# Moving the x chain's weight pool from the left side of SBUF to the right end

## The chip, the core and the metric

The kernel runs on one core of one Trainium2 chip. The metric is the device time of one execution in microseconds; less is better. Before the change the median of three executions is 1627.95 us (1626.01 to 1629.65). The profile was taken of one further execution.

## The reference

A block of two layers (a mixer of windowed attention and a state space model, then sparse attention) on x, 256 tokens of width 1024, is followed by a block of two layers in which x attends to a context `ctx` of 256 tokens. In the second block both streams are normalised and modulated by a conditioning vector, and each layer ends in a gated feed-forward of width 2816; the second layer's mixer is a bidirectional SSM. All is float32. Cut to what matters here:

```
h = x
for layer in range(2):                       # first block, x alone
    hn = rms_norm(h, norm_g[layer])
    h = h + (even_layer if layer == 0 else odd_layer)(hn, ...)   # hn @ w_in ... @ w_out
x = h
for i in range(2):                           # second block, x and ctx
    h, hc = modulate(x, ...), modulate(ctx, ...)
    y, yc = attention_mixer(h, hc, ...) if i == 0 else ssm_mixer(h, hc, ...)
    x = x + g1 * y
    x = x + g2 * swiglu(modulate(x, ...), w_gate, w_up, w_down)
    if i == 0:
        ctx = ctx + cg1 * yc
        ctx = ctx + cg2 * swiglu(modulate(ctx, ...), w_gate, w_up, w_down)
return rmsnorm(x, final_norm_g)
```

Nearly all of the arithmetic is in products of a 256 x 1024 (or 2816, or 2048) activation with a weight matrix that is read once from DRAM.

## The kernel before

**Two chains.** The x chain (both blocks) and the ctx chain (its attention, its feed-forward, and its part of the SSM layer) are written as one program, and a scheduler interleaves them by priority. Each chain has its own weight pool, its own activation pools and its own PSUM tiles: `psx` for x (PSUM banks 0 to 3), `psc` for ctx (banks 4 to 7).

**Weights.** A `Weights` object (L156) is a pool with three kinds of buffer, each 128 partitions x 1024 float32, so 4096 bytes in each partition: `raw` for what a DMA of the SP queue brings (`fetch`, L167), and `h` and `l`, the two halves of the number in the rounded format of TensorE. `load` (L175) makes `h` on ScalarE (L181) and `l = raw - h` on VectorE (L182), now and then on GpSimd. `wx`, the x chain's pool, has 3 raw, 2 h and 2 l buffers: 7 x 4096 = 28672 bytes in a partition. `wc`, the ctx chain's, has 2 of each: 24576 bytes. Activations are split the same way into a pair of tiles (`nhx`/`nlx` the normalised x, `nhc`/`nlc` the normalised ctx, `fh`/`fl` the inner activations of a feed-forward, `yH`/`yL`, `oHx`/`oLx`, `ysH`/`ysL` the outputs of the mixers), and a product is the sum of three matmuls: high x high, low x high, high x low.

**Which operand is loaded.** TensorE holds one operand (128 columns, loaded by LDWEIGHTS) and streams the other past it. In the profile `out<-a,b` is a matmul that streams `a` past the loaded `b`. There are two forms:
- `feat_tiles` (L273) loads a 128 x 128 slice of the weights and streams 256 tokens of activation: `pffnx<-nhx,h` (gate and up products of the x feed-forwards, 24 matmuls for each tile of weights), `pcvx` (SSM input products; for three of four channel tiles also with `nhc`/`nlc` streamed past the same x weights), `pg` (gates of the first block, 16 tiles), and a few more (`pu`, `pqi`, `pki`, `pglu`, 14 tiles together). `pffnc<-nhc,h` is the same of the ctx feed-forward, with weights of `wc`.
- `tok_step` (L232) loads a slice of activation and streams 512 or 256 columns of weights: `pdx<-h,nhx`, `pdx<-h,fh`, `pdx<-h,ysH` and so on for x, `pdc<-h,nhc`, `pdc<-h,oHc`, `pdc<-h,fh` for ctx. The outputs `pdx` lie in `psx`, apart from half of the product with `ysH`/`ysL`, which lies in `psc`.

`step_sizes` (L1216) is a small case of the first form, with 64 weight columns in place of 128 (`pdt`, in `psx` for x).

**Order of the program around the change.** The scheduler's order is fixed when the program is built. The pools are stacks: left pools grow from byte 0 of each partition, right pools from the end. On the left stand `con`, `res`, `act`, `wk`, then `wx`, `xw` and one pool for each stage of the x chain (`ev`, `od`, `l0`, `ff0`, `l1`, `ff1`); on the right `wc`, then `cx`, which are closed by `cst.close()` (L1479) ahead of the x chain's SSM stage, whose pool `l1` then grows over their place. Start bytes in each partition, of the built program before:

| tile | pool | start byte |
|---|---|---|
| `nhx`, `yH`, `oHx` | act | 36512 |
| `nlx`, `yL`, `oLx` | act | 44704 |
| `nhc`, `oHc` | act | 52896 |
| `nlc`, `oLc` | act | 61088 |
| first buffer of `wx` | wx | 70048 |
| `fh`, `fl` of x | ff0, ff1 | 115104, 126368 |
| `ysH`, `ysL` | l1 | 115232, 131616 |
| `fh`, `fl` of ctx | cx | 165664, 191264 |
| first buffer of `wc` | wc | 204768 |

The other buffers of `wx` and `wc`, and the slices of 128 or 256 columns of any of these tiles, follow at multiples of 512 bytes from these starts.

Of the kernel before, what the change touches and what calls it, by code (L numbers as in the profile page):

```python
# [47 lines left out]
WX = (3, 2)  # L48
WC = (2, 2)
# [42 lines left out]
def build(tc, A):  # L92
    nc = tc.nc
    T, V, S, G, SY = nc.tensor, nc.vector, nc.scalar, nc.gpsimd, nc.sync
    es = ExitStack()
# [8 lines left out]
    def pool(name, bufs=1, space=None, right=False):  # L104
        kw = {"side": "right"} if right else {}
        if space is not None:
            kw["space"] = space
        else:
            kw["reuse_waits"] = "tile"
        return tc.tile_pool(name=name, bufs=bufs, **kw)  # L110
# [5 lines left out]
    class Banks:  # L116
        def __init__(self, name, bufs):
            self.p = es.enter_context(pool(name, 1, PS))
            self.bufs = bufs
            self.k = name[2]  # L120
# [33 lines left out]
    flip = misc[:, 420:548]  # L154

    class Weights:  # L156
        def __init__(self, name, raw, hl, eng, right=False):
            self.p = (cst if right else es).enter_context(pool("w" + name, raw, right=right))
            self.hl = hl
            self.eng = eng  # L160

            self.ahead = []
            self.n = 0
            self.name = name
            self.on_pool = 0
# [21 lines left out]
    def cols(a, ncols, n0, k0=0, kt=8):  # L187
        return [(lambda t: t, dram(a, k0 * 128 * ncols + n0, [[ncols, 128], [128 * ncols, kt], [1, 128]]))]

    wx = Weights("x", *WX, SY)  # L190
    cst = ExitStack()
    wc = Weights("c", *WC, SY, right=True)
    cx = cst.enter_context(pool("cx", right=True))
    xw = es.enter_context(pool("xw"))
    xpool = {"x": (xw, "xn"), "c": (cx, "cfl")}
# [1312 lines left out]
```

## Time and profile before

| | |
|---|---|
| median of three executions | 1627.95 us (1626.01 to 1629.65) |
| profiled execution | 1627.45 us |
| its span, first to last instruction | 1625.4 us |
| mean granted TensorE clock | 0.973 of full |
| PE busy | 94% of the span |
| VectorE, ScalarE, GpSimd busy | 68%, 46%, 19% |
| DMA | 264.58 MB, mean 163 GB/s |

The span lies 2.05 us under the execution's own time, and that under the median by 0.50 us. PE is TensorE's matmuls, PEld its weight loads, which overlap them; DVE is VectorE, ACT ScalarE, POOL GpSimd, SP the queue that issues the DMAs. Matmuls are pipelined: the length that the profile gives to one is longer than the distance from one start to the next, and it is the distance that adds up to time.

### The profile page before, as it was taken

To read this page: it belongs to the slowest core of one execution; us is meant where nothing else is said; L and a number is where in the kernel's file an instruction comes from. 1 tells how busy PE (TensorE), PEld (TensorE's weight loads), DVE (VectorE), ACT (ScalarE), POOL (GpSimd) and SP (SyncE) were. 2 spreads that over 40 slices of the span, in tenths; PEclk is the share of its full clock that TensorE was granted. 3 is DMA by queue.
4 is the path that set the end of the run, shared out by engine and by line. 5 is a ranking of instruction groups with operands and counts; after the bars stand their busy time and mean duration, and the time that the engine had idled before them with its cause. 6 is when DMAs were issued, how large, how long until landed. Compare 5 with 4: busy or idle time off the path is not lost.

```text
span 1625.4 us, 27122 instructions
## 1 busy us (share of the span) xinstructions
PE 1524.9 (94%) x10660; PEld 1307.0 (80%) x10660; DVE 1104.7 (68%) x1823; ACT 745.3 (46%) x1336; POOL 301.8 (19%) x260
## 2 busy tenths in 40 slices
PE   6989987999999999999999999887999999899998
PEld 5655664786998988888889897787899889699997
DVE  6789776567766676655666565569888787655666
ACT  3412256545544544666444343433454444444443
POOL 4476420000100100000000000129454430100000
PEclk9989998999999999999999999889999999999999
DMA  8755574466656656423665766334444433555664
GB/s 264 216 183 170 167 202 138 124 179 209 185 178 205 197 175 194 138 79 95 200 206 183 235 185 204 99 90 131 106 119 117 113 97 114 162 162 176 192 185 136
DMA packets 302735, 264.58 MB, mean 163 GB/s; under 512 B 27329, under 2 KB 256495, under 8 KB 302608
## 3 DMA queue, kind: packets, MB, share of 16 engines
q1 hardware_dynamic: 301680, 259.70, 53.5%
q0 software_dynamic: 928, 3.15, 0.7%
q8 instruction: 84, 1.38, 0.3%
q14 instruction: 43, 0.35, 0.1%
HBM read 261.47 MB, written 1.34 MB: 162 GB/s over the span
## 4 chain that ended last, share of the span: by engine, by line
PE 77%; DVE 7%; DMA 7%; POOL 5%; issue 2%; ACT 1%; SPq 1%; POOLq 0%; DVEq 0%; ACTq 0%
PE pdx L132 21%; PE pffnx L132 16%; PE pffnc L132 8%; PE pdc L132 7%; PE pcvx L132 6%; PE pada L905 3%; DMA araw<-ada_w 2%; PE pg L132 2%; PE py L132 2%; PE pl0x L132 1%; POOL EW L1372 1%; PE pl1x L132 1%; PE pocx L132 1%; PE ptcx L1086 1%; DVE l L182 1%
## 5 line engine op out<-in xcount | busy, mean ns | idle before, releaser
L182 DVE TENSOR_TENSOR l<-raw,h 128x1024 fp32r<-128x1024 f32 (+2 forms) x362 | 452.9, 1254 | 284.8 <-ACT h L181 231.1
L181 ACT ACTIVATE h<-raw 128x1024 fp32r<-128x1024 f32 (+2 forms) x374 | 389.2, 1042 | 487.3 <-PE pdx L132 147.5
L132 PE MATMUL pffnx<-nhx,h 128*128 128x256 f32 x704 | 174.9, 286 | 0.0
L132 PE MATMUL pffnx<-nlx,h 128*128 128x256 f32 x704 | 174.7, 285 | 0.2 <-DVE nlx L352 0.2
L132 PEld LDWEIGHTS pffnx<-nhx,h 128*128 128x128 f32 x704 | 136.5, 194 | 1.2 <-issue 1.2
L132 PEld LDWEIGHTS pffnx<-nlx,h 128*128 128x128 f32 x704 | 136.3, 194 | 1.0 <-DVE nlx L352 0.9
L310 POOL TENSOR_TENSOR sums<-sums,nhalf 128x1 f32<-128x1 f32 x20 | 14.6, 730 | 559.0 <-DVE sums L306 542.0
L132 PE MATMUL pffnx<-nhx,l 128*128 128x256 f32 x704 | 99.0, 283 | 0.0
L905 PE MATMUL pada<-araw,cT 128*32 128x256 f32 x704 | 76.3, 403 | 18.5 <-DMA araw<-ada_w 18.5
L132 PEld LDWEIGHTS pffnx<-nhx,l 128*128 128x128 f32 x704 | 91.1, 193 | 0.0
L132 PE MATMUL pffnc<-nhc,h 128*128 128x256 f32 x352 | 87.1, 285 | 0.0
L132 PE MATMUL pcvx<-nhx,h 128*128 128x256 f32 x256 | 77.3, 309 | 9.3 <-DVE cv L1257 9.3
L182 POOL TENSOR_TENSOR l<-raw,h 128x1024 fp32r<-128x1024 f32 (+1 forms) x12 | 27.3, 2277 | 315.7 <-PE pdx L132 202.2
L132 PE MATMUL pffnc<-nlc,h 128*128 128x256 f32 x352 | 85.5, 281 | 0.0
L132 PE MATMUL pdx<-h,nhx 128*128 128x256 f32 (+1 forms) x256 | 83.6, 345 | 0.4 <-DVE cv L1257 0.4
L132 PE MATMUL pdx<-h,nlx 128*128 128x256 f32 (+1 forms) x256 | 80.7, 334 | 0.0
L132 PE MATMUL pdx<-h,fh 128*128 128x256 f32 (+1 forms) x264 | 78.8, 323 | 0.0
L132 PE MATMUL pdx<-h,fl 128*128 128x256 f32 (+1 forms) x264 | 77.8, 319 | 0.0
L132 PE MATMUL pcvx<-nlx,h 128*128 128x256 f32 x256 | 75.3, 302 | 0.0
L132 PEld LDWEIGHTS pffnc<-nhc,h 128*128 128x128 f32 x352 | 66.4, 189 | 2.8 <-issue 1.2
L132 PEld LDWEIGHTS pffnc<-nlc,h 128*128 128x128 f32 x352 | 66.4, 189 | 0.8 <-DVE ss L408 0.4
L132 PEld LDWEIGHTS pcvx<-nhx,h 128*128 128x128 f32 x256 | 51.8, 203 | 13.3 <-issue 13.1
(600 smaller groups left out, 3892.4 us busy)
## 6 DMA issues: line engine op xcount, KB each, us to landing
araw<-ada_w SPq DMA_DIRECT2D x88, 512.0 KB
raw<-ffn_w_gate SPq DMA_DIRECT2D x66, 512.0 KB
raw<-ffn_w_up SPq DMA_DIRECT2D x66, 512.0 KB
raw<-ffn_w_down SPq DMA_DIRECT2D x54, 512.0 KB
raw<-ssm_w_in SPq DMA_DIRECT2D x48, 512.0 KB
raw<-od_w_in SPq DMA_DIRECT2D x25, 512.0 KB
raw<-attn_w_qkv SPq DMA_DIRECT2D x24, 512.0 KB
raw<-attn_w_o SPq DMA_DIRECT2D x32, 256.0 KB
```

Source lines behind the costliest of these rows:

```text
L132: i = T.matmul(out, l, r, start=start, stop=stop)
L181: S.activation(h[:, :n], raw[:, :n], AF.Copy)
L182: (G if self.on_pool > 0 else V).tensor_tensor(l[:, :n], raw[:, :n], h[:, :n].bitcast(F32), op=ALU.subtract)
L310: G.tensor_tensor(s[:, 3:4], s[:, j - 1:j], nhalf[:, 0:1], op=ALU.pow)
L905: T.matmul(pt[32 * q:32 * q + 32, 0:256], cT[:, k, :], raw[:, q * 256:(q + 1) * 256], start=k == 0, stop=k == 7, tile_position=(0, 32 * q))
L1086: T.transpose(pt[:, e, r], P[:, e, r, ki * 128:(ki + 1) * 128], ident)
L1372: (G if CWP else V).tensor_tensor(EW, E, W, op=ALU.mult)
```

## The change

`wx` becomes a right pool, opened before `wc`, so that it takes the last 28672 bytes of the partition; `wc` and `cx` stand left of it. `wx` stays open to the end of the kernel, on the stack `es`; `wc` is closed with `cst` as before.

```diff
@@ -154,8 +154,8 @@
     class Weights:
-        def __init__(self, name, raw, hl, eng, right=False):
-            self.p = (cst if right else es).enter_context(pool("w" + name, raw, right=right))
+        def __init__(self, name, raw, hl, eng, stack):
+            self.p = stack.enter_context(pool("w" + name, raw, right=True))
             self.hl = hl
             self.eng = eng
@@ -187,9 +187,9 @@
-    wx = Weights("x", *WX, SY)
     cst = ExitStack()
-    wc = Weights("c", *WC, SY, right=True)
+    wx = Weights("x", *WX, SY, es)
+    wc = Weights("c", *WC, SY, cst)
     cx = cst.enter_context(pool("cx", right=True))
```

In the built program no instruction, no place in any engine's order and no wait differs: only the start bytes of SBUF tiles do. `con`, `res`, `act` and `wk` stay. The first buffer of `wx` goes from byte 70048 to byte 200672. Every other tile (the x chain's `xw` and stage pools, `wc` and `cx`) moves down by 28672 bytes, so that what overlapped of `l1` and the closed ctx pools overlaps as before.

## Rows read from the trace of the kernel before

**Rows 1.** The page, busy time by engine: us, share of the span, instructions.

```profile
PE 1524.9 (94%) x10660; PEld 1307.0 (80%) x10660; DVE 1104.7 (68%) x1823; ACT 745.3 (46%) x1336; POOL 301.8 (19%) x260
```

**Rows 2.** The page, the chain that ended last: shares of the span by engine and line.

```profile
PE 77%; DVE 7%; DMA 7%; POOL 5%; issue 2%; ACT 1%; SPq 1%; POOLq 0%; DVEq 0%; ACTq 0%
PE pdx L132 21%; PE pffnx L132 16%; PE pffnc L132 8%; PE pdc L132 7%; PE pcvx L132 6%; PE pada L905 3%; DMA araw<-ada_w 2%; PE pg L132 2%; PE py L132 2%; PE pl0x L132 1%; POOL EW L1372 1%; PE pl1x L132 1%; PE pocx L132 1%; PE ptcx L1086 1%; DVE l L182 1%
```

**Rows 3.** Windows: stretch, length; busy us of PE, PEld, DVE, ACT, POOL; clock, DMA share, GB/s.

```profile
400.00:500.00 100.00, 100.00 (x742) 90.07 (x742) 73.51 (x139) 51.23 (x89) 6.73 (x10) 1.00 0.60 179
...
690.00:756.00 66.00, 66.00 (x488) 54.69 (x488) 38.94 (x79) 42.23 (x92) 0.00 (x0) 1.00 0.25 73
840.00:890.00 50.00, 50.00 (x419) 50.00 (x418) 31.16 (x45) 22.93 (x34) 0.00 (x0) 1.00 0.61 184
...
1100.00:1330.00 230.00, 208.77 (x1562) 198.01 (x1562) 193.77 (x298) 104.53 (x196) 121.24 (x100) 0.96 0.43 114
```

**Rows 4.** The chain in order of time: start, length in us, piece, number of instructions.

```profile
410.05 5.55 PE pffnc L132 x47
...
431.15 6.24 PE pffnc L132 x53
...
441.44 20.15 PE pg L132 x168
...
463.76 7.96 PE pffnc L132 x70
...
478.65 7.71 PE pffnc L132 x65
...
492.45 5.47 PE pffnc L132 x48
...
1523.47 63.36 PE pffnx L132 x528
```

**Rows 5.** Timeline of PE: start, us from first start to last end, instructions in one run.

```profile
141.59 1.09 PE L132 MATMUL pdc<-l,nhc 128*128 128x512 f32 x4
...
446.06 1.12 PE L132 MATMUL pg<-nhx,l 128*128 128x256 f32 x8
...
465.43 1.07 PE L132 MATMUL pffnc<-nhc,l 128*128 128x256 f32 x8
...
1048.35 1.07 PE L132 MATMUL pdt<-nhx,l 128*64 128x256 f32 x8
...
1397.04 1.10 PE L132 MATMUL pdx<-l,ysH 128*128 128x512 f32 x4
...
1499.76 1.07 PE L132 MATMUL pdx<-l,fh 128*128 128x512 f32 x4
```

**Rows 6.** Weight loads by tile and window: count, ns shortest/median/longest, first and last start.

```profile
L132 PEld LDWEIGHTS pffnc<-nhc,h x73: 186/188/192, 690.0 to 755.9; 128*128 128x128 f32 x73
...
L132 PEld LDWEIGHTS pcvx<-nhc,h x137: 187/192/331, 1111.4 to 1329.7; 128*128 128x128 f32 x137
...
L132 PEld LDWEIGHTS pdx<-h,ysL x56: 187/188/192, 1372.2 to 1413.8; 128*128 128x128 f32 x56
...
L132 PEld LDWEIGHTS pdx<-h,fl x66: 187/192/193, 1492.5 to 1522.7; 128*128 128x128 f32 x66
...
L132 PEld LDWEIGHTS pffnx<-nhx,h x176: 191/192/193, 1523.2 to 1585.3; 128*128 128x128 f32 x176
```

**Rows 7.** The page's groups: count, busy us, mean ns of one, idle time before them.

```profile
L132 PE MATMUL pffnx<-nhx,h 128*128 128x256 f32 x704 | 174.9, 286 | 0.0
...
L132 PE MATMUL pcvx<-nhx,h 128*128 128x256 f32 x256 | 77.3, 309 | 9.3 <-DVE cv L1257 9.3
...
L132 PE MATMUL pcvx<-nhc,h 128*128 128x256 f32 x192 | 56.4, 294 | 0.0
```

**Rows 8.** VectorE's low halves in the ctx window 690:760 and the x window 827:891.

```profile
L182 DVE TENSOR_TENSOR l<-raw,h x10: 1215/1220/1225, 689.4 to 755.5; 128x1024 fp32r<-128x1024 f32 x10
...
L182 DVE TENSOR_TENSOR l<-raw,h x21: 1224/1225/1227, 830.5 to 888.2; 128x1024 fp32r<-128x1024 f32 x21
```

## The prediction

> **What bounds the kernel now.** First the busy shares: PE works 94% of the span, so the matmuls' pace is the first suspect [rows 1]. Then the chain of waits, which says which of them set the end: 77% of the span is PE, led by the x chain's `pdx` (21%) and `pffnx` (16%); DMA and VectorE have 7% each [rows 2]. Then the windows: in an x feed-forward (840:890) PE and its weight loads are both busy all of the time while VectorE, ScalarE and DMA have slack [rows 3]. The pace of PE is then the time.
>
> Since the change moves nothing but addresses, the question is whether the trace holds anything that depends on where a tile lies. It does. The chain in order of time gives the distance of matmuls in unbroken runs of the same shape (128 x 128 loaded, 256 columns streamed): x takes 63.36 us for 528, 120.0 ns each, and 20.15 us for 168 in `pg`, 119.9; ctx takes 113.7 (7.96 us for 70), 114.0, 117.7, 118.1 and 118.6 in five runs, 32.93 us for 283 together, **116.4 ns** [rows 4]. Eight in a row show it at a glance: 1.12 us for x, 1.07 for ctx [rows 5]. Weight loads have a median of 192 ns in `pffnx` and 188 in `pffnc` [rows 6], at a clock of 1.00 in both windows [rows 3].
>
> **What makes the difference.** Four things differ between the chains: the activations, the PSUM banks, the stage, and the bytes where operands start. The start bytes of the table, divided by 256, leave these remainders: 160 for all activations in `act`, 160 for `wx`, 224 for `wc`, 160 for the x `fh`/`fl`, 32 for `ysH`/`ysL` and for the ctx `fh`/`fl`. Slices are multiples of 512 bytes on, so every slice keeps its tile's remainder. Now read the rows by pair:
> - streamed and loaded operand with the same remainder (160 and 160): 192 ns in `pffnx`, in `pdx<-h,fl`, and in `pcvx<-nhc,h`, which streams ctx activations past x weights [rows 6]. So it is not the activations.
> - different remainders: 188 in `pffnc` (160 and 224), and 188 in `pdx<-h,ysL` (160 and 32) [rows 6]. That last pair streams the same `wx` buffers as `pdx<-h,fl`, from tiles that begin 128 bytes apart on the left side, half of them in x's own banks. So it is neither the banks nor the side.
> - `pdt`, with half as many columns loaded, from `wx` into x's banks, has the quick 1.07 us for eight [rows 5]: the banks again don't forbid the quick pace, and a shorter load lifts the delay.
>
> I read this as the two reads of PE, the streamed operand and the next load, getting in each other's way most when they start at the same place in a block of 256 bytes. This is worked out from the rows, not shown by one alone.
>
> **The change part by part.** `wx` goes to byte 200672, remainder 224, what `wc` has. 28672 is 112 x 256, so all tiles that move by it keep theirs. Every x product whose pair was 160/160 becomes 224/160 or 160/224, which are ctx's pairs today. Against the profiled execution's 1627.45 us (0.50 under the median):
>
> 1. *x weights loaded, 256 columns streamed.* Gain of one: 120.0 - 116.4 = 3.6 ns, between 2.3 (the run at 117.7) and 6.3 (the run at 113.7) [rows 4]. I take the mean of five runs since both paces occur. `pffnx`: 3 x 704 = 2112 matmuls [rows 7], 253 us at 120.0, and the chain holds 16% of 1625.4 = 260 [rows 2]: all of it is path. 2112 x 3.6 = **-7.6 us**. `pcvx`: 3 x 256 + 3 x 192 = 1344 [rows 7], 161 us, of which the chain holds 6% = 98, so 0.61: in the SSM stage PE is busy 208.77 of 230 us and waits on GpSimd and DMA for the rest [rows 3]. 1344 x 3.6 x 0.61 = **-3.0 us**. `pg`: 16 tiles x 24 = 384, 46 us, on the chain 2% = 33, so 0.71: **-1.0 us**. The small ones: 14 x 24 = 336, at the same 0.71: **-0.9 us**.
> 2. *x weights streamed (`pdx`).* With 512 columns a run of four takes 1.07 us at 160/160 (`fh`), and 1.09 at 224/160 (ctx's `pdc<-l,nhc`); 1.10 at 160/32 (`ysH`) [rows 5]. So the long ones get slower, by 0.02 us over three distances, 7 ns, or by nothing, as the start bytes also set how a run falls in; half of it, 3 ns, for 744 matmuls (the code's count without `ysH`) is **+2.2 us**. With 256 columns there are 1248 of them; I take the smallest gain of part 1, 2.3 ns: **-2.9 us**. Bounds: +5.2 and 0 at one end, 0 and -7.9 (6.3 ns) at the other.
> 3. *`ysH`/`ysL`*: 160/32 becomes 224/32, both unequal: 0.
> 4. *Conversions.* VectorE's `l` has a median of 1220 ns on `wc` and 1225 on `wx` [rows 8]; 5 ns of some 270 is 1.4 us, and it hides behind PE in the feed-forwards; the whole of it has 1% of the chain [rows 2]. 0.
> 5. *Transfers.* Packets of 512 bytes fill `wc` in 690:756 and `wx` in 840:890. Share x 16 engines / rate gives 28.1 ns for one (0.25, 73 GB/s) and 27.2 (0.61, 184) [rows 3], 3% more at remainder 224, within the rounding of 0.25. DMA has 7% of the chain, 2% of that `araw`, which keeps its remainder; 3% of the other 81 us is 2.4 us at most, and most of the transfers land while PE is busy: **+0.3 us**, between 0 and 2.4. If the cover went, a feed-forward tile would need 0.61 of the 2.9 us that its 24 matmuls take; that is far off.
>
>    [...]
>
> Sum: -7.6 - 3.0 - 1.0 - 0.9 + 2.2 - 2.9 + 0.3 = -12.9, so 1614.6; rounded, **1614.5 us**. What is late next: in the feed-forwards still PE, at 2.8 us a tile; in the SSM stage the GpSimd, DMA and VectorE steps, counted in the 0.61.
>
> **The rivals.**
> - *Placement does nothing* (0.12). The pace would belong to ctx's banks, or to its broken-up runs. For it: no ctx product runs in x's banks, and no unbroken ctx run is longer than 70. Against it: `pdt` and `ysL`, above. Time: 1627.45 + 0.3, 1627.8. [...]
> - *Only the long products feel it* (0.05). If the 256-column pace belongs to the banks, but 512 columns do suffer from unequal remainders, as 1.10 and 1.09 against 1.07 suggest, 744 x 7 to 10 ns = 5.2 to 7.4 us is added: **1633 to 1635**, slower. In general this side wins when part 1 yields less than about 2 ns for each of some 3400 path matmuls.
> - *Packets into `wx` get dearer and nothing is gained* (0.03). The rounding of 0.25 and 0.61 allows at most 28.8 against 26.9 ns [rows 3], 7% more, and 7% of the 81 us of part 5, if all of it were path into `wx`, is 5.7 us: **1633**, slower. It decides where the pace of PE stays as it is. Against it: most transfers land under a busy PE. [...]
> - There is no rival in which another wait takes over: no wait, no order and no overlap of pools changes.
>
> **How the numbers follow.** The forecast has 0.80. Its own range: all at 2.3 ns (-7.9 for part 1), part 2 and 5 at their worse bounds, gives -0.3; all at 6.3 ns (-21.7), part 2 at its best, -29.6. Both ends at once are unlikely; 1605 to 1622 holds it in nine of ten. To hold 8 in 10 over all cases the range goes up to the no-change case: **1605 to 1627.5**. A measurement of this kernel can tell 0.2%, 3.3 us, from no change. Faster: 0.80 less the forecast's own thin end, 0.79. Within 0.2%: the first rival and that thin end, 0.13. Slower: the other two, 0.08.
>
> **What would show it.** Right: weight loads of `pffnx`, `pcvx` and `pg` at 188 ns; runs of eight at 1.07 or 1.10 us; the 528 of a feed-forward in 60 to 62 us instead of 63.4; `pdx<-h,ysL` unchanged. `pcvx` gains less on the chain than its pace. Wrong: `pffnx` still at 120.0 ns and 192 means the remainder is not the cause; `pffnx` quicker but the end not nearer means the path lay elsewhere; `pdx` runs of four at 1.10 or more with 256-column products unchanged is the slower rival.

## The result and the profile after

The changed kernel takes **1610.76 us** (median of four executions, 1610.01 to 1614.37); the kernel before takes 1628.05 on the same chip (1626.01 to 1629.65). The ratio is **0.9899, 95% interval 0.988 to 0.9918**: 17.3 us less, between 13 and 20. In a second comparison, below, the same program took 1612.7 us, ratio 0.9909 [0.9893, 0.9925]; one of its five executions took 3707 us, and the ratio is of the other four. The profiled execution after has a span of 1608.0 us, 17.4 under the one before. Forecast were 1614.5 us and a gain of 12.9.

The page of the kernel after: busy time by engine, and the shares of the chain.

```profile
PE 1506.7 (94%) x10660; PEld 1287.5 (80%) x10660; DVE 1102.8 (69%) x1823; ACT 746.7 (46%) x1336; POOL 303.4 (19%) x260
...
PE 78%; DVE 6%; DMA 6%; POOL 5%; issue 2%; ACT 1%; SPq 1%; POOLq 0%; ACTq 0%; DVEq 0%
PE pdx L132 21%; PE pffnx L132 15%; PE pffnc L132 8%; PE pdc L132 7%; PE pcvx L132 6%; PE pada L905 3%; DMA araw<-ada_w 3%; PE pg L132 2%; PE py L132 2%; PE pl0x L132 1%; POOL EW L1372 1%; PE pl1x L132 1%; PE pocx L132 1%; PE ptcx L1086 1%; PE pv L132 1%
```

The busy time of PE fell by 18.2 us with the same 10660 matmuls [rows 1]; VectorE, ScalarE and GpSimd each stayed within 2 us. The chain's shares hardly moved [rows 2]: PE does the same work a little quicker, and no wait came in for it.

The chain of the kernel after in order of time (start, length, piece, number of instructions).

```profile
309.24 5.44 PE pdx L132 x48
...
538.95 5.86 PE pdx L132 x48
...
438.41 19.79 PE pg L132 x168
...
460.38 7.96 PE pffnc L132 x70
...
823.51 61.44 PE pffnx L132 x520
...
921.76 62.40 PE pffnx L132 x528
...
1153.65 3.76 PE pcvx L132 x33
...
1417.81 59.25 PE pffnx L132 x519
...
1507.13 62.19 PE pffnx L132 x528
```

The pace is the distance from start to start. The piece of 168 `pg` now takes 117.8 ns each (119.9 in [rows 4]), the four runs of `pffnx` 118.2, 118.2, 114.2 and 117.8, while the ctx piece of 70 that nothing should change still takes 7.96 us [rows 4]. **The four runs are not alike** (each of the two feed-forwards has two): by the starts, past its opening, one stands at 113.3 and three at 117.8, and each holds its pace for hundreds of matmuls; before, all four stood at 120.0. Here is what answers to it in the chain of the kernel before, for pieces not shown yet.

```profile
312.90 5.75 PE pdx L132 x48
...
541.63 5.94 PE pdx L132 x48
...
1163.77 3.94 PE pcvx L132 x33
```

The pieces of 48 `pdx` of 256 columns (five in either chain) went from 28.94 us together to 27.84, 120.6 to 116.0 ns each; of the eight pieces of 33 `pcvx` of either chain, seven now take 3.76 us and one 3.94, where all took 3.94 to 4.01.

Weight loads after, over the whole span where no window is named (`ysL` 1355:1412, `fl` 1476:1508).

```profile
L132 PEld LDWEIGHTS pffnx<-nhx,h x704: 186/188/192, 818.6 to 1567.9; 128*128 128x128 f32 x176
...
L132 PEld LDWEIGHTS pcvx<-nhc,h x192: 187/188/336, 1037.2 to 1341.9; 128*128 128x128 f32 x192
...
L132 PEld LDWEIGHTS pdx<-h,ysL x60: 187/188/190, 1355.6 to 1401.8; 128*128 128x128 f32 x60
L132 PEld LDWEIGHTS pdx<-h,fl x66: 187/188/188, 1476.9 to 1506.4; 128*128 128x128 f32 x66
```

All medians are 188 now; the three that stood at 192 in [rows 6] came down, `ysL` stayed. A load of 188 does not tell the pace, though: the run at 113.3 and those at 117.8 each have that median. The timeline has the long products:

```profile
1385.02 1.10 PE L132 MATMUL pdx<-l,ysH 128*128 128x512 f32 x4
...
1484.22 1.08 PE L132 MATMUL pdx<-l,fh 128*128 128x512 f32 x4
```

Four with `fh` take 1.08 us for 1.07, with `ysH` 1.10 as before [rows 5]. Last, an x feed-forward among the windows, and VectorE's low halves in the ctx window 686:752.

```profile
835.00:885.00 50.00, 50.00 (x426) 49.98 (x425) 31.14 (x45) 23.87 (x35) 0.00 (x0) 1.00 0.62 186
...
L182 DVE TENSOR_TENSOR l<-raw,h x9: 1217/1225/1226, 686.1 to 744.3; 128x1024 fp32r<-128x1024 f32 x9
```

50 us hold 426 matmuls for 419 [rows 3], at the same granted clock. 0.62 x 16 engines x 512 bytes / 186 GB/s is 27.3 ns a packet, as before (27.2); 14787 of the window's 15887 packets hold 512 bytes, and their mean in the trace is 27.8 ns in both (840:890 before): packets into `wx` at remainder 224 are no dearer. The 5 ns of `l` in [rows 8] were not the place either: ctx, whose weights kept their remainder, has a median of 1225 now. In both profiles its window holds some at 1215 to 1217 and some at 1224 to 1226, and a median of nine or ten falls to either side.

### The profile page after: what moved, and what is told of

Its sections match the earlier page's. It is cut to its first block, busy times and chain, and to the rows that moved or that the text cites. A ratio compares the mean times of both kernels' runs of the same rounds, so it can differ in the third digit from the quotient of the medians.

```text
span 1608.0 us, 27122 instructions
## 1 busy us (share of the span) xinstructions
PE 1506.7 (94%) x10660; PEld 1287.5 (80%) x10660; DVE 1102.8 (69%) x1823; ACT 746.7 (46%) x1336; POOL 303.4 (19%) x260
## 4 chain that ended last, share of the span: by engine, by line
PE 78%; DVE 6%; DMA 6%; POOL 5%; issue 2%; ACT 1%; SPq 1%; POOLq 0%; ACTq 0%; DVEq 0%
PE pdx L132 21%; PE pffnx L132 15%; PE pffnc L132 8%; PE pdc L132 7%; PE pcvx L132 6%; PE pada L905 3%; DMA araw<-ada_w 3%; PE pg L132 2%; PE py L132 2%; PE pl0x L132 1%; POOL EW L1372 1%; PE pl1x L132 1%; PE pocx L132 1%; PE ptcx L1086 1%; PE pv L132 1%
## 5 line engine op out<-in xcount | busy, mean ns | idle before, releaser
L132 PE MATMUL pffnx<-nlx,h 128*128 128x256 f32 x704 | 169.1, 281 | 0.8 <-DVE nlx L352 0.7
L132 PE MATMUL pffnx<-nhx,h 128*128 128x256 f32 x704 | 169.1, 280 | 0.0
L132 PEld LDWEIGHTS pffnx<-nlx,h 128*128 128x128 f32 x704 | 132.9, 189 | 1.9 <-DVE nlx L352 1.8
L132 PEld LDWEIGHTS pffnx<-nhx,h 128*128 128x128 f32 x704 | 133.0, 189 | 0.8 <-issue 0.8
```

The lines of the kernel that those rows point to most:

```text
L132: i = T.matmul(out, l, r, start=start, stop=stop)
```

## The experiments

**1. The remainder without the side.** Two empty tiles around `wx` in the kernel before, nothing else:

```diff
-    wx = Weights("x", *WX, SY)
-    cst = ExitStack()
+    es.enter_context(pool("pada")).tile([128, 16], F32, name="pada"); wx = Weights("x", *WX, SY)
+    cst = ExitStack(); es.enter_context(pool("padb")).tile([128, 48], F32, name="padb")
```

> wx stays on the left side, 64 bytes further on (remainder 224 of 256), and nothing else changes its remainder. Theory (the remainders of the streamed operand and of the next loaded one must differ): as the changed kernel, 1611 us, within 3, and weight loads of pffnx at 188 ns. Rival 'side' (the place at the right end is what helps): as before, 1628 us, weight loads at 192 ns.

Measured: 1614.55 us (1612.74 to 1616.43), ratio 0.9918 [0.989, 0.9946], weight loads of `pffnx` at 188 ns. That is 3.6 us above the 1611 of the expectation, which allowed 3, but the gain is there without any move to the right.

**2. The side without the remainder.** The same two tiles (64 and 192 bytes) around `wx` in the changed kernel, on the right, so that `wx` starts at 160 again.

> wx stays at the right end beside wc, but 64 bytes lower, so that it has the remainder 160 of the activations again; wc and all others keep theirs. Theory: as before the change, 1628 us, within 3, pffnx at 120.0 ns each and its weight loads at 192 ns. Rival 'side': as the changed kernel, 1611 us and 188 ns.

Measured: 1626.3 us (1623.62 to 1628.74), ratio 0.9992 [0.9978, 1.0005]. The gain is gone, with `wx` where the change put it but for 64 bytes. Its chain and its weight loads:

```profile
1524.71 63.36 PE pffnx L132 x528
...
L132 PEld LDWEIGHTS pffnx<-nhx,h x704: 186/192/331, 820.6 to 1586.6; 128*128 128x128 f32 x176
```

That is the kernel before to the hundredth of a microsecond [rows 4, 6]. In both, PE has the order of the kernel before. The two runs together settle it: within the noise of some 3 us the remainder is the whole of the gain, and the side none of it.

**3. The other operand moved.** The kernel before with 64 bytes ahead of `act` and 192 behind it.

> wx stays where it was before (remainder 160); the activations in act go 64 bytes on instead, to 224, which is what wc has. Theory (the relation of the two operands counts): pffnx, pcvx and pg gain as in the changed kernel, some 14 us together, pdx with fh gains nothing, and pffnc, now 224 with 224, loses: weight loads 192 ns and 120 ns a matmul, 982 x 3.6 = 3.5 us; in all 1615 us, within 3. Rival 'own place' (wx does well at 224 and badly at 160, whatever it meets): 1628 us, pffnx at 192 ns and pffnc still at 188.

Measured: 1622.89 us (1618.89 to 1628.2), ratio 0.9976 [0.9958, 0.9993]. Chain and weight loads:

```profile
461.50 8.39 PE pffnc L132 x70
...
926.40 62.38 PE pffnx L132 x528
...
L132 PEld LDWEIGHTS pffnc<-nhc,h x352: 186/192/239, 387.8 to 766.1; 128*128 128x128 f32 x176
```

In kind as the theory had it: with `wx` untouched `pffnx` leaves 120 ns, and ctx, whose weights were not touched either, falls to 8.39 us for 70 (119.9 ns) and to loads of 192. So it is the relation of the two operands. In size it missed: 5 us instead of 13. No run of `pffnx` found the quick pace here, all stand at 117.8, and the long products with `nhx` and `nlx`, which stream `wx` at 160 past 224, became slower: `pdx<-l,nhx` went from 228.9 ns to 233.6 (means of neighbouring starts, gaps left out).

**4. The pace by itself.** A kernel of nothing but matmuls, each group 288 of them (144 with 512 columns), in one execution. A distance is the start byte of the streamed operand less that of the loaded one, modulo 256.

> Leaves out all of the computation: it only runs matmuls back to back, with no DMA beside them, 288 for each distance between the start bytes of the streamed and of the loaded operand: 0, 32, 64 to 224 bytes, with 256 columns (qa to qh) and with 512 (ra to rh, 144 each), and 0, 64, 128, 192 with the loaded one at another remainder (sa, sc, se, sg). Theory: only distance 0 (qa, sa) has 120.0 ns and weight loads of 192; all others lie between 113 and 118.5 ns with loads at 188; with 512 columns distance 0 has the least, 226 to 229, the others 229 to 234. Rival 'not the bytes' (DMA traffic, banks or the kernel's other engines make the difference): all distances alike within 1 ns.

Its chain in order of time:

```profile
57.61 34.55 PE pqa L40 x288
...
126.08 33.92 PE pqc L40 x288
160.00 34.55 PE pqd L40 x288
194.55 34.18 PE pqe L40 x288
...
262.90 33.92 PE pqg L40 x288
...
330.90 32.69 PE pra L40 x144
...
397.19 32.97 PE prc L40 x144
...
531.10 33.60 PE prg L40 x144
...
598.29 34.55 PE psa L40 x288
...
700.95 32.69 PE psg L40 x288
```

With no transfer of data, and no engine beside TensorE but VectorE, which copies eight columns behind every 24 matmuls, the effect is all there: 34.55 / 288 = 120.0 ns at distance 0 (`qa`, `sa`). Three things differ from my expectation. A distance of 96 (`qd`) is as bad as 0, and yet its weight loads have a median of 188, so not every slow pair shows the 192. At 192, that is -64, the same distance gave 117.8 in one place (`qg`) and **113.5** in another (`sg`). And with 512 columns the sign counts: 227.0 at 0 (`ra`), 229.0 at +64 (`rc`), 233.3 at -64 (`rg`). The operands' start bytes alone made 227.0 into 233.3 and 113.5 into 120.0.

**5. A distance of 128 bytes.** As experiment 1, with 128 and 128 bytes.

> wx on the left side at remainder 32, which lies 128 bytes from the activations' 160. Theory 'distance' (the pace goes by the distance between the two start bytes as the bare matmuls showed it: 118.7 ns at 128 with 256 columns, 233.4 with 512, against 120.0 and 228 at distance 0): 4104 + 1201 short products x 1.1 ns = -5.8 us, 684 long ones x 5 ns = +3.4, and the 186 long ones with ysH and ysL (32 too, now equal) x 6 ns = -1.1; -3.5 in all, so 1624 us. Rival 'any difference does': as with wx at 224, 1611 to 1615 us.

Measured: 1623.69 us (1622.06 to 1627.0), ratio 0.9981 [0.9969, 0.9994]: as the bare matmuls foretold, and 9 us behind `wx` at 224 in experiment 1. That two start bytes differ is not enough.

**6. The other 64 bytes.** As experiment 1, with 192 and 64 bytes.

> wx on the left side at remainder 96, 64 bytes from the activations as in the changed kernel, but on the other side of them. Theory 'distance with its sign': products that stream activations past wx are now at +64 (117.7 ns: 4104 x -2.1 ns = -8.6 us), those that stream wx at -64 (256 columns 116 ns: 1201 x -3.7 = -4.4; 512 columns 233.4: 684 x +4.9 = +3.4); -9.6 in all, so 1618 us, 4 to 7 above the changed kernel. Rival 'any difference of 64 does': 1611 to 1615 us, as with wx at 224.

Measured: 1614.62 us (1612.43 to 1618.98), ratio 0.9921 [0.9896, 0.9946]. This does not tell the two apart: it is the rival's number, and the interval reaches to the theory's. The trace shows the signs at work on the long products: four of `pdx<-l,fh` (-64) take 1.09 us, four of `pdx<-l,ysH` (+64 here) 1.07 to 1.08, where the changed kernel has 1.08 and 1.10. In total the signs trade against each other. One thing fits neither: the last run of `pffnx`, at +64 here, stands at 113.3 ns, the other three at 117.8.

```profile
1514.81 59.84 PE pffnx L132 x528
```

**7. The raw buffers left behind.** The changed kernel with the three raw buffers of `wx` in a pool of their own at remainder 160, `h` and `l` at 224.

```diff
...
-            self.p = stack.enter_context(pool("w" + name, raw, right=True))
+            self.r = stack.enter_context(pool("r" + name, raw, right=True)); ... ; self.p = ... if name == "x" else self.r
...
-            raw = self.p.tile([128, 1024], F32, tag="raw", name="raw")
+            raw = self.r.tile([128, 1024], F32, tag="raw", name="raw")
```

> As the changed kernel, but the three raw buffers, into which the DMAs write and from which no matmul reads, have their own pool at remainder 160; the h and l buffers keep 224. Theory (only the operands of TensorE count): as the changed kernel, 1611 us, within 3. Rival 'part of the change is in the transfers or conversions' (packets dearer at 224): up to 2.4 us less than the changed kernel; if the raw buffers brought part of the gain, more: up to 1628.

Measured: 1612.51 us (1609.79 to 1613.08), ratio 0.9902 [0.9886, 0.9918], the changed kernel's own. Neither the transfers nor the reads of `raw` by ScalarE and VectorE have a part in it that the interval, 2.6 us either way, would show. By the starts its four runs of `pffnx` stand at 117.8, 117.8, 113.3 and 117.8, as in the changed kernel; the third shows it in a window past its opening, 40 us for 355 matmuls:

```profile
1435.00:1475.00 40.00, 40.00 (x355) 40.00 (x354) 25.49 (x38) 20.09 (x30) 0.00 (x0) 1.00 0.66 192
```

Those of experiment 1 (59.15 us for 520, 62.40 for 528, 59.25 for 519 and 62.19 for 528) stand at 113.3, 117.8, 113.3 and 117.8. So which pace a run finds is not fixed by the remainders.

**8. Two paces.** Bare matmuls in runs of 24, each after a pause, or broken by one matmul of another kind.

> Leaves out all of the computation: bare matmuls of 256 columns in short runs of 24, each run after a pause, for eight distances (qa to qh: 0 to 224 in steps of 32), and runs at -64 (ya to yf) and +64 (za to zf) broken by one odd matmul: 128, 192, 320 or 512 columns, or 256 columns with equal remainders or with a loaded operand 128 bytes off. Theory 'two paces' (at some distances a run keeps the pace into which its start puts it): at -64 both 113.3 and 117.8 occur, each held for a whole run, and some breaker switches between them; at +64 117.8 nearly always; at 0 always 120.0. Rival 'one pace for each distance': every run of one distance has the same mean within 1 ns, whatever came ahead of it.

Of 40 runs straight after a pause at -64, 33 stood at 113.3 to 114.0 ns and 7 at 117.6 to 117.8 (mean distance from the fourth start on); at +64 38 of 40 at 117.8; at 0 all ten at 119.4 to 120.0. At -64 one matmul of 128 columns turned 113.3 into 117.8 or back at 14 of 15 places; one of 192 left all 15 runs behind it at 113.3. At +64 the other two starts stood at 113.3, and none of the pieces led away from 117.8. The two-pace theory stands; one pace for each distance does not.

**9. Choosing the pace.** At -64, put into the slow pace first, then a product of 256 columns cut in two.

> Leaves out all of the computation: bare runs of 24 matmuls of 256 columns at -64 (streamed 160, loaded 224). Each group starts after a pause, is then put into the slower pace by one matmul of 128 columns, and then meets the same odd piece three times, 24 matmuls behind each: one matmul of 192 columns (ya), or one product of 256 columns cut in two: 192+64 (yb), 64+192 (yc), 128+128 (yd), 224+32 (ye), 32+224 (yf), 96+160 (yg), 160+96 (yh). Theory 'two paces': each run of 24 is at 113.3 or at 117.8 throughout, and at least one of the pieces leads into 113.3 from either, so that a kernel can choose its pace. Rival 'chance': whatever the piece, both paces follow in turn, or the slower one stays.

The timeline of one group each: 192 columns alone (`ya`), 224+32 (`ye`), 160+96 (`yh`).

```profile
55.80 3.04 PE L33 MATMUL pya<-mv,st 128*128 128x256 f32 x24
...
58.77 3.01 PE L33 MATMUL pya<-mv,st 128*128 128x256 f32 x24
...
61.71 2.93 PE L33 MATMUL pya<-mv,st 128*128 128x256 f32 x24
...
356.23 3.04 PE L33 MATMUL pye<-mv,st 128*128 128x256 f32 x24
359.11 0.29 PE L41 MATMUL pye<-mv,st 128*128 128x224 f32 x2
359.25 2.99 PE L33 MATMUL pye<-mv,st 128*128 128x256 f32 x24
...
582.48 3.04 PE L33 MATMUL pyh<-mv,st 128*128 128x256 f32 x24
585.36 0.32 PE L41 MATMUL pyh<-mv,st 128*128 128x160 f32 x2
585.51 3.05 PE L33 MATMUL pyh<-mv,st 128*128 128x256 f32 x24
```

The first run of each is the slow one, ahead of the piece: 117.8 ns by the starts, from the fourth on. The lengths hold the first and last matmuls too, so the starts tell more. Behind `ye`'s cut they are 113.2 to 113.5 ns apart, in all five groups; behind 192+64, 64+192, 128+128, 32+224 and 96+160 they are 113.5 to 114.1, and 160+96 leaves them at 117.8 in four of five. (In five of these 35 groups the run ahead of the first piece had not stayed in the slow pace: it stood at 113.8.) 192 columns alone led out at the second piece. Where the parts are 224 and 32 or 160 and 96 columns, the second part also starts 128 bytes off modulo 256; with 192, 64 and 128 it does not, and those lead to the quick pace as well. A cut has its price: the 24 products behind `ye`'s take 2.82 us from their first start (359.25) to that of the next cut (362.07), where 24 x 113.3 are 2.72; what is lost lies ahead of the fourth start.

**10. A kernel that does it.** First the changed kernel again, as the base:

> The changed kernel once more, as the base for the next two on the same chip: 1611 us, within 3. Its feed-forwards may differ from those of its first profile by the pace that each falls into (59.9 or 62.2 us for 528); theory and rivals say the same here.

Measured: 1612.7 us, ratio 0.9909 [0.9893, 0.9925]. A window in each of its four runs of `pffnx`:

```profile
840.00:880.00 40.00, 40.00 (x356) 40.00 (x355) 26.34 (x37) 19.41 (x31) 0.00 (x0) 1.00 0.67 197
930.00:980.00 50.00, 50.00 (x427) 50.00 (x426) 30.93 (x45) 24.01 (x36) 0.00 (x0) 1.00 0.65 185
1435.00:1475.00 40.00, 40.00 (x355) 40.00 (x355) 26.40 (x38) 19.47 (x31) 0.00 (x0) 1.00 0.68 197
1520.00:1560.00 40.00, 40.00 (x342) 40.00 (x341) 25.14 (x36) 18.97 (x29) 0.00 (x0) 1.00 0.65 188
```

The first and the third stand at 113.3 ns, the second and the fourth at 117.8: two slow runs, where the first profile of the same program had three.

Then with 24 cuts:

```diff
-                mm(out, wh[:, k], al, False, False)
+                for c in ((slice(0, 224), slice(224, 256)) if k == 1 and mark in CUT else (slice(0, 256),)):
+                    mm(out[:, c], wh[:, k], al[:, c], False, False)
```

with `CUT` holding the marks of the feed-forward's columns of weights 0, 1, 6, 11, 12 and 17.

> The changed kernel, and in each x feed-forward half a dozen of the 352 products that stream nlx past h are cut into 224 and 32 columns (24 cuts in all, 26 ns each = 0.6 us). Theory 'two paces' (a cut leads into 113.3 ns, which holds until the run is broken): all four unbroken runs of pffnx take 59.9 us for 528 plus the cuts, where three of four take 62.2 now: 3 x 2.3 - 0.6 = 6 us less than the changed kernel, 1604 to 1605 us. Rival 'chance': the paces stay mixed, 1611 to 1612 us. Rival 'other bound': at 113.3 ns the weights don't arrive in time, gaps open in pffnx and the runs stay at 61 us or more.

Measured: **1605.85 us** (1601.1 to 1607.75), ratio to the kernel before 0.9865 [0.9847, 0.9883], clear of the base's interval.

```profile
823.61 59.71 PE pffnx L132 x525
...
920.12 60.86 PE pffnx L132 x534
...
1414.03 59.88 PE pffnx L132 x524
...
1503.98 60.55 PE pffnx L132 x534
```

All four runs are at the quick pace: 241.00 us for 2117 pieces, 113.8 each with the cuts, and 113.3 by the starts past the openings. PE has no gaps there (each run is one piece of the chain, and PE is busy 190.60 of 190.60 us from 823.6 to 1014.2), so at this pace no transfer becomes the bound. Medians differ by 6.9 us; 6 were expected. But two things stand between that and what the cuts bring. One is a term that I had wrong. The timeline of PE at a cut:

```profile
920.52 0.29 PE L132 MATMUL pffnx<-nlx,h 128*128 128x224 f32 x2
920.66 0.36 PE L132 MATMUL pffnx<-nhx,h 128*128 128x256 f32 x1
920.86 0.28 PE L132 MATMUL pffnx<-nlx,h 128*128 128x256 f32 x1
```

I had counted the two parts alone, 0.14 us to the next start, 26 ns more than an uncut product. The product behind them takes 0.20 us: 0.34 for two that take 0.23 at the quick pace, so a cut costs some **110 ns**, 24 of them 2.7 us. Two runs that go from 117.8 to 113.3 are worth 2 x 528 x 4.5 = 4.8 us, so the pace nets some 2. From first start to last the four runs take 246.6 us in the base and 242.8 here, 3.8 less; the rest of that lies in their openings, which differ between executions: those of the base's first and third run fall into stretches with a granted clock of 0.50 (824.95 to 828.37 and 1412.05 to 1425.7 us), behind others in which PE was busy 1.72 of 2.95 us (from 822) and 4.52 of 7.05 (from 1405); that the one brings the other is not shown.

The other is the order of the program. In experiments 1 to 3 and 5 to 7 PE has the order of the kernel before. Here the scheduler, which sets the order when the program is built, put 145 of the 8548 matmuls outside `pffnx` in other places, all of them in the SSM stage (1069.6 to 1161.4 us). That stage, from the first to the last weight load of `pcvx<-nhx,h`, took 305.1 us here, 311.0 in the base, and 305.8 in the first profile of the base's own program. So the kernel is faster and the quick pace of all four runs is shown; how much of the other 3 us comes from the new order, and how much is chance, is not. Fewer cuts were not tried.

**11. The SSM stage too.** One product of each `pcvx` tile is cut in the same way.

> As the last, and one product of each of the 32 pcvx tiles is cut too (0.8 us). Theory: pcvx goes from 115.3 ns to 113.4 on average, 1279 x 1.9 = -2.4, so 1.5 us less than with the cuts in the feed-forwards alone: 1603 us. Rival 'the SSM stage is bound elsewhere': no gain from it, or 0.8 us more.

Measured: **1603.14 us** (1600.28 to 1604.99), ratio 0.9851 [0.9838, 0.9865], the fastest kernel of the study. Against the cuts in the feed-forwards alone this is 2.7 us less by the medians, but the intervals overlap, so a gain of this part is not shown. By the price just found, 32 cuts cost 3.5 us, more than the 2.4 that the pace can give. What the medians have beyond that has a rival that no run takes apart: the order changed far more here (1278 of the 8548 matmuls outside `pffnx` stand in other places, the cut-off pieces not counted), and the SSM stage took 297.7 us for the 305.1 of experiment 10.

## Why the prediction was right, and where its sizes were off

What the prediction rests on was right: the pace goes by the start bytes of the streamed and the loaded operand (experiments 1 to 4). The reading behind it, two reads that get in each other's way, was my estimate; what happens inside TensorE stays open. That the same place in a block of 256 bytes is the worst holds in part: with 256 columns 96 bytes are as slow as 0 (120.0 ns), and with 512 columns equal start bytes are the quickest (227.0 ns). The rows of the kernel before bear out the 256: `nhx` and `wx` start 256 bytes apart modulo 512, `fl` and `wx` at the same place, and both have loads of 192 ns; `ysL` and `wx`, equal modulo 128 but not 256, have 188 [rows 6]. The prediction's remark that a shorter load lifts the delay rests on `pdt` alone, whose starts are 116.3 ns apart with 64 columns loaded; no run varied the load. By its steps, with the means of neighbouring starts of one product, gaps left out, in the first profile and in the second (experiment 10):

1. *x weights loaded.* `pffnx`: forecast 3.6 ns for each of 2112, from ctx's mean. Measured from 120.0: 3.3 with three of four runs at 117.8, 4.45 with two of four, so -7.0 and -9.4 us for -7.6. Ctx's mean of 116.4 was a mixture of two paces, as the prediction said; what it did not see is that an unbroken run keeps one of them to its end, so that four long runs are four draws. `pcvx`: 119.6 became 115.3 and 116.1, 4.3 and 3.5 ns for 3.6 forecast; with the share of 0.61 on the path, which no run tested, that makes -3.6 and -2.9 us for -3.0. `pg` and the small ones: 3.1 to 3.8 ns at a share of 0.71, -1.8 and -1.7 us for -1.9.
2. *x weights streamed.* This step was off most. With 256 columns I took "the smallest gain of part 1, 2.3 ns"; the pieces of 48 gained 4.6 (120.6 to 116.0), but all of them together 3.9 and 3.7 (119.8 to 115.9 and 116.1), -4.8 and -4.6 us for -2.9. With 512 columns the loss is 229.0 - 227.0 = 2.0 ns by the bare matmuls, 1.8 in the kernel (228.5 to 230.3), some +1.5 us for +2.2. That the start bytes also set how a run falls in, which the forecast allowed for, was an estimate that no run took apart.
3. *`ysH`/`ysL`*: 1.10 and 188 before and after, as said.
4. *Conversions* and 5. *transfers*: nothing, by experiment 7 and by 27.3 against 27.2 ns; +0.3 was forecast.

With the measured sizes the sum is -7.0 - 3.6 - 1.8 - 4.8 + 1.5, some **-15.7 us**, and -17.1 in the second profile; the two comparisons of medians gave 17.3 and 14.5, either within the other's interval. In the first profile the 2.8 us between the sum and the forecast are step 2 (-1.9 - 0.7), `pcvx` (-0.6) and the transfers (-0.3), less what `pffnx` (0.6) and `pg` with the small ones (0.1) fell short by. That the forecast came as near as this is luck in part: one run of `pffnx` that draws the other pace is worth 528 x 4.5 ns = 2.4 us, and the two profiles of one program differ by such a draw.

The signs that were named came: 188 everywhere, which does not tell the pace; 62.40 and 62.19 us for 528, just past the "60 to 62", as three of four took the slower pace; `pdx<-h,ysL` unchanged; and `pcvx` may have brought less than its pace: 1344 x 4.3 ns would be 5.8 us, and the stage from the first to the last weight load of `pcvx<-nhx,h` went from 309.7 us (1043.8 to 1353.5) to 305.8, with its short `pdx` in it. But in the second profile of the same program it took 311.0, so its length moves by 5 us by itself, and what `pcvx` brought on the path is not shown.

*The rivals.* "Placement does nothing" falls with experiments 1 and 2, and its cause with 4: one set of banks, unbroken runs, and still 113.5 to 120.0. "Only the long products feel it" had its part: they do lose, 2 ns at +64. The change escaped the worse price by its sign, which the prediction did not consider: at -64 it would have been 6.3 ns by the bare matmuls. "Packets get dearer" falls with 7 and the 27.3 ns.

## What to carry to other kernels

Where matmuls follow each other without gaps and the granted clock is full, take the distance of their starts from the chain, and if the same shape has two distances in one kernel, compare the start bytes of the streamed and of the next loaded operand modulo 256: with 256 columns equal ones cost 120.0 ns here where 113.3 is to be had, with 512 columns equal ones were the quickest, at 227.0; and an empty tile of 64 bytes ahead of a pool moves all of it (experiment 1). Test the side, the banks and the bytes apart: an empty tile ahead and another behind move one pool and leave the rest alone. Where a run of some hundred matmuls sits at the slower of two paces, products cut in two can lead it into the quicker: with six cuts in each, all four runs of `pffnx` stood at 113.3 ns, where two of the base did. A cut costs some 110 ns, about what the quick pace gives a run of 24 (24 x 4.5). A cut changes the program, so compare the engines' order before and after: where the scheduler has changed it too, the gain is not the cut's alone.

## What the runs showed that I had not expected

- The distance is not a matter of equal or not. For 256 columns: 120.0 ns at 0 and 96 bytes, 118.7 at 128 and 160, 118.3 at 224 and some 117.8 at 32 in the bare runs; 117.8 at +64, seldom 113.3; 113.3 or 117.8 at -64. For 512: 227.0 at 0, 229.0 at +64, 233 to 234 at the others.
- At -64 there are two paces that hold for as long as the run is unbroken (519 matmuls in 59.25 us and 528 in 62.40 in one execution), and one matmul of another width can turn one into the other (one of 128 columns at 14 of 15 places). Why is open: the runs show the pattern, not the mechanism inside TensorE.
- The bare runs at +64 took 117.8 but for two of 40. Yet one of four runs of `pffnx` in experiment 6, at +64, held 113.3 for 528 matmuls, and the short `pdx` of the changed kernel, also at +64, have pieces at 5.44 / 48 = 113.3. The `pdx` stream each slice of weights past several loads, which the bare runs did not; whether that is the reason was not tried.
